# Mixture-of-experts kernel on one core: the arms for an expert's second and third token block are reordered, their jumps are hinted on TensorE, and an unused operand is no longer written

## The chip, the cores and the metric

The kernel runs on one core of one Trainium2 chip. The metric is the device time of one execution in microseconds (us), lower is better.

## What is computed

The reference is a two-layer diffusion backbone over 1024 latent and 256 context tokens of width 1024. Each layer does token mixing (gated linear attention, differential attention, pooling) and then a mixture of 16 experts. Only the experts matter here: every token goes to two experts of one group, and each expert is a gated feed-forward net.

```python
def expert_block(args):
    xblk, e = args
    return (jax.nn.silu(xblk @ w1[e]) * (xblk @ w3[e])) @ w2[e]
...
out = jnp.zeros((n_tok + 1, d), h.dtype).at[slot_tok].add(yb * slot_w[:, None])
```

How many tokens an expert gets is known only at run time, since the router decides it from the data.

## The kernel before

**Experts.** One stage per layer goes through the 16 experts in the order `eo`, written out one after the other in the program. An expert's weights come as 12 units of 128x1024. SyncE loads each (`fetch`, 8 buffers ahead), ScalarE copies it into the first half of a buffer `ew` and VectorE, or GpSimd for every third unit, subtracts to get the low part in the second half (L1579 and L1581, in `load_unit`); `ew` has 13 buffers. All matmuls are done three times, with high and low parts (`mm3`, L67 to L69).

**Token blocks.** Tokens are taken in blocks of 128. Block 0 always runs (`block` on `x0`: 72 matmuls of 128x512). Blocks 1 and 2 depend on the count `cnt` of the expert, which each engine loads into a register (L1814, L1872): a second block up to 64 tokens goes through `block_half`, a larger one through `block`; the same holds for the third. A loop follows for more than 384 tokens.

**Order.** The arms of an expert run before its block 0. Inside block 0, at the steps `side(u)`, the 12 weight units of the next expert are loaded, each when TensorE has let go of a unit of this expert, and the next expert's token blocks are gathered and prepared (`prep`). So an expert with at most 128 tokens has two blocks 0 in a row on TensorE. Here an expert is called N (none of the arms runs), H (half block), F (one full block) or T (a full block and a half block); the layers have the orders T and N in turn first, more N and H later. By the scatters and blocks in the trace, of 32 experts 16 are N, 7 H, 2 F and 7 T.

**Branches.** Each engine runs its own copy of the branches. In the program the code of an arm that is skipped lies between the branch and its target:

```python
with tc.If(cnt > P + P // 2) as big:      # L1822
    ...                                   # block 1; L1832: third block, full; L1834: loop
    with big2.Else():                     # L1853
        with tc.If(cnt > 2 * P):          # L1854: third block, half
with big.Else():
    with tc.If(cnt > P):                  # L1857: second block, half
        block_half(...)
```

So an N expert jumps at L1822 over everything up to the `Else`, and there at L1857 over the half block. An H expert jumps at L1822 and then runs the half block.

**Preparation.** `prep` transposes a block of tokens on TensorE, splits it into high and low parts (`split`, ScalarE and VectorE at L63 and L64), and on VectorE writes the low part of the first 64 tokens once more beside the high part (L1611). Only `block_half` reads that copy.

Of the kernel before, what the change touches and what calls it, by code (L numbers as in the profile page):

```python
# [20 lines left out]
P = 128  # L21
D = 1024
KD = D // P
NCTX = 256
# [31 lines left out]
def backbone_kernel(ctx: ExitStack, tc: tile.TileContext, x, ctx_in, cond, w_mod, b_mod, norm1, norm2, w_in_t, w_in_vg,  # L56
                    w_in_vd, w_out, wa2, gla_norm, lam_v, diff_norm, pool_w, pool_scale, router_w, router_b,
                    experts, final_norm, consts, rope, slot0, levels, edges, out, dbg=None, depth=DEPTH):
    nc = tc.nc
# [88 lines left out]
    for l in range(depth):  # L148
        last = l == DEPTH - 1
# [1403 lines left out]
        with ExitStack() as st:  # L1553
# [5 lines left out]
            early = True  # L1559
            xg2 = mp1.tile([P, D], F32, name="xg2")  # L1560
            g2b = {}
            for c in ((0,) if last else (0, 1)):
# [37 lines left out]
                fetch()  # L1600
            xt_ = [[mp1.tile([P, KD, n], F32R, name=f"x{n}{i}") for n in (P + P // 2, P)] for i in range(3)]

            def prep(g, xt):
                xh, xl = xt[0][:, :, P // 2:], xt[1]

                def half(j, tag="xtp"):
                    tp = pm_.tile([P, 4, P], F32, name="xtp", tag=tag, bufs=1 if tag == "xtp" else 2)
                    for i in range(4):
                        nc.tensor.transpose(tp[:, i, :], g[:, (4 * j + i) * P:(4 * j + i + 1) * P], ident)
                    split(xh[:, 4 * j:4 * j + 4, :], xl[:, 4 * j:4 * j + 4, :], tp)  # L1610
                    nc.vector.tensor_tensor(out=xt[0][:, 4 * j:4 * j + 4, 0:P // 2], in0=tp[:, :, 0:P // 2],  # L1611
                                            in1=xh[:, 4 * j:4 * j + 4, 0:P // 2].bitcast(F32), op=OP.subtract)
                return half

            def gain(n, w, wc):
# [112 lines left out]
            def col(e, b):  # L1728
                return slice(b * NE + e, b * NE + e + 1)

            def idle(u):
                pass

            for b in (1, 0):
                pf = prep(gg[b], xt_[2 * b])
                pf(0, ("hps", "xtp")[b])
                pf(1, ("hpse", "hpse")[b])
            units += [load_unit(u) for u in range(7, NUNIT)]
# [72 lines left out]
                        out_op(j)  # L1811
                    nc.sync.dma_start(out=out[P + 7 * P:2 * P + 7 * P, :], in_=X[7])

            cnt = nc.values_load(cnt_i[0:1, eo[0]:eo[0] + 1], min_val=0, max_val=cap)  # L1814
            gg[0] = gather(ix[:, col(eo[1], 0)], "xg0")
            gg[1] = gather(ix[:, col(eo[1], 1)], "xg1")
            if early:
                nc.gpsimd.indirect_dma_start(out=xg2, out_offset=None, in_=h2s,
                                             in_offset=bass.IndirectOffsetOnAxis(ap=ix[:, col(eo[0], 2)], axis=0))
            for ei, e in enumerate(eo):  # L1820
                x0, x1, x2 = xt_[ei % 2], xt_[2], xt_[(ei + 1) % 2]
                with tc.If(cnt > P + P // 2) as big:  # L1822
                    if not early:
                        nc.gpsimd.indirect_dma_start(out=xg2, out_offset=None, in_=h2s,
                                                     in_offset=bass.IndirectOffsetOnAxis(ap=ix[:, col(e, 2)], axis=0))
                    p2 = prep(xg2, x2)

                    def side1(u):
                        if u in (10, 11):
                            p2(u - 10, ("xtp", "hpse")[u - 10])  # L1830
                    block(x1, units, sw[:, col(e, 1)], swc[:, col(e, 1)], yx[:, col(e, 1)], side1, "e")
                    with tc.If(cnt > 2 * P + P // 2) as big2:  # L1832
                        block(x2, units, sw[:, col(e, 2)], swc[:, col(e, 2)], yx[:, col(e, 2)], idle, "e")
                        with tc.If(cnt > 3 * P):  # L1834
                            for t in tiles:
                                for j in range(2):
                                    nc.gpsimd.indirect_dma_start(
                                        out=slots, out_offset=bass.IndirectOffsetOnAxis(ap=di[:, t, j:j + 1], axis=0),
                                        in_=sva[:, t, j, 1:4], in_offset=None)
                            with tc.For_i(e * cap + 3 * P, e * cap + cnt, P) as i:  # L1840
                                sd = wk.tile([P, 3], F32, name="sd", tag="sd", bufs=1)
                                nc.sync.dma_start(out=sd, in_=slots[bass.ds(i, P), :])
                                si = wk.tile([P, 2], I32, name="si", tag="si", bufs=1)
                                nc.vector.tensor_copy(out=si, in_=sd[:, 0:2])
                                p3 = prep(gather(si[:, 0:1], "yt"), x1)
                                p3(0)
                                p3(1)
                                if not last:
                                    nc.vector.tensor_scalar(out=sd[:, 0:1], in0=sd[:, 0:1], scalar1=float(NCTX), scalar2=None, op0=OP.is_lt)
                                    nc.vector.tensor_tensor(out=sd[:, 1:2], in0=sd[:, 0:1], in1=sd[:, 2:3], op=OP.mult)  # L1850
                                    nc.vector.tensor_tensor(out=sd[:, 2:3], in0=sd[:, 2:3], in1=sd[:, 1:2], op=OP.subtract)
                                block(x1, units, sd[:, 2:3], sd[:, 1:2], si[:, 1:2], idle, "e")
                    with big2.Else():  # L1853
                        with tc.If(cnt > 2 * P):  # L1854
                            block_half(x2, units, sw[:, col(e, 2)], swc[:, col(e, 2)], yx[:, col(e, 2)])
                with big.Else():
                    with tc.If(cnt > P):  # L1857
                        block_half(x1, units, sw[:, col(e, 1)], swc[:, col(e, 1)], yx[:, col(e, 1)])
                nxt = []
                nx = {}  # L1860

                def side(u):
                    if ei + 1 == NE:
                        return
# [3 lines left out]
                    if early and u == 1:  # L1868
# [155 lines left out]
```

## Time and profile before

| what | value |
|---|---|
| runs (3) | median 2896.91 us, 2889.07 to 2903.89 |
| the profiled execution | 2908.22 us, span 2906.5 us |
| TensorE busy | 2539.1 us, 87% |
| VectorE busy | 1816.5 us, 63% |
| ScalarE busy | 1241.8 us, 43% |
| GpSimd busy | 898.9 us, 31% |
| mean granted TensorE clock | 0.934 |
| mean DMA rate | 170 GB/s |

The span is the time from the first to the last instruction of the profiled execution. Busy shares are means over stages with different limits, and a matmul at half clock counts as busy for twice as long.

### The profile page before, as it was taken

The numbers are of one execution on the slowest core, as the hardware profiler recorded it, in microseconds if no ns is written. First come the engines' busy times: TensorE is split into PE (matmuls) and PEld (weight loads), VectorE is DVE, ScalarE is ACT, GpSimd is POOL, SyncE is SP. The second block draws the span as 40 slices with busy tenths as digits, with TensorE's granted clock in tenths as the row PEclk, the third lists the DMA queues.
The fourth block names the chain that finished last, engine by engine and source line by source line (L and its number), as shares of the span: only waits on it lengthen the run. The fifth ranks groups of instructions, "written<-read, shape, count | busy, mean of one in ns | idle before, by whom it ended". The sixth has DMA issues, their size and how long they took to land. (4 is left out here: it accounts for less than half of the span.)

```text
span 2906.5 us, 41486 instructions
## 1 busy us (share of the span) xinstructions
PE 2539.1 (87%) x15412; PEld 2132.5 (73%) x15412; DVE 1816.5 (63%) x3175; ACT 1241.8 (43%) x2060; POOL 898.9 (31%) x576
## 2 busy tenths in 40 slices
PE   6999998898896899889887999979989788878875
PEld 3878887787785677667766898868978666656664
DVE  3304765777478667766775227748857866656765
ACT  3322213566234555544554232137743354545443
POOL 0000113302245444544540001122014445545452
PEclk8999999999897999989998999989989899989987
DMA  8373128331225666776774342173122568686765
GB/s 291 126 246 123 70 86 200 64 71 44 103 109 213 226 223 220 256 252 202 244 243 161 125 141 88 70 181 84 37 89 102 224 222 285 202 279 232 249 234 182
DMA packets 159573, 494.06 MB, mean 170 GB/s; under 512 B 18896, under 2 KB 40016, under 8 KB 158768
## 3 DMA queue, kind: packets, MB, share of 16 engines
q1 hardware_dynamic: 110336, 361.14, 37.5%
q0 software_dynamic: 29312, 99.39, 11.8%
q10 hardware_dynamic: 19552, 28.84, 2.7%
q8 instruction: 200, 3.28, 0.5%
q14 instruction: 173, 1.42, 0.2%
HBM read 408.75 MB, written 79.15 MB: 168 GB/s over the span
## 5 line engine op out<-in xcount | busy, mean ns | idle before, releaser
L1581 DVE TENSOR_TENSOR ew<-eraw,ew 128x1024 fp32r<-128x1024 f32 x256 | 433.7, 1713 | 65.2 <-ACT ew L1579 60.1
L1579 ACT ACTIVATE ew<-eraw 128x1024 fp32r<-128x1024 f32 x384 | 390.5, 1054 | 132.4 <-PE hps L69 115.0
L67 PE MATMUL hps<-ew,x 128*128 128x512 f32 x656 | 281.9, 430 | 105.2 <-PEq L1857 100.6
L1581 POOL TENSOR_TENSOR ew<-eraw,ew 128x1024 fp32r<-128x1024 f32 x128 | 334.4, 2622 | 61.1 <-ACT ew L1579 36.1
L212 PE MATMUL ps<-hh,w 128*128 128x256 f32 x2096 | 289.3, 292 | 17.9 <-ACT hh L319 4.7
L212 PEld LDWEIGHTS ps<-hh,w 128*128 128x128 f32 x2096 | 269.0, 197 | 27.7 <-issue 7.9
L69 PE MATMUL hps<-ew,x 128*128 128x512 f32 x656 | 271.2, 413 | 8.3 <-DVE x L64 7.6
L68 PE MATMUL hps<-ew,x 128*128 128x512 f32 x656 | 271.8, 414 | 0.0
L962 DVE TENSOR_REDUCE mx<-S 128x1 f32<-128x1280 f32 (+1 forms) x144 | 196.8, 1370 | 108.2 <-PE S L957 106.8
L1627 POOL DMA_INDIRECT xb<-yt,yx x54 | 131.2, 2430 | 368.6 <-DVE yt L1626 206.0
L67 PEld LDWEIGHTS hps<-ew,x 128*128 128x128 f32 x656 | 132.6, 202 | 139.7 <-issue 105.7
L970 ACT ACTIVATE pe<-S,mx 128x1280 f32<-128x1280 f32 (+1 forms) x144 | 177.4, 1232 | 49.2 <-DVE mx L962 41.2
L956 PE MATMUL S<-kk,qh 128*128 128x512 f32 (+1 forms) x400 | 159.0, 398 | 16.7 <-DMA qh<-qs 8.3
L69 PEld LDWEIGHTS hps<-ew,x 128*128 128x128 f32 x656 | 132.2, 202 | 41.7 <-DVE x L64 10.2
L68 PEld LDWEIGHTS hps<-ew,x 128*128 128x128 f32 x656 | 133.2, 203 | 28.2 <-issue 1.1
L212 PE MATMUL ps<-hl,w 128*128 128x256 f32 x1048 | 149.1, 286 | 0.0
L67 PE MATMUL ps<-wv,hh 128*128 128x256 f32 (+1 forms) x480 | 142.3, 296 | 0.0
L957 PE MATMUL S<-kk,ql 128*128 128x512 f32 (+1 forms) x400 | 141.4, 368 | 0.3 <-DMA ql<-qs 0.3
L69 PE MATMUL yps<-ew,ghl 128*128 128x512 f32 x328 | 132.5, 404 | 8.0 <-DVE ghl L64 8.0
L67 PE MATMUL yps<-ew,ghl 128*128 128x512 f32 x328 | 138.4, 422 | 0.0
L69 PE MATMUL ps<-wv,hl 128*128 128x256 f32 (+1 forms) x480 | 138.1, 288 | 0.0
L68 PE MATMUL ps<-wv,hh 128*128 128x256 f32 (+1 forms) x480 | 137.9, 287 | 0.0
(597 smaller groups left out, 5765.1 us busy)
## 6 DMA issues: line engine op xcount, KB each, us to landing
eraw<-in_experts_dram SPq DMA_DIRECT2D x384, 512.0 KB
s<-in_w_mod_dram SPq DMA_DIRECT2D x91, 512.0 KB
raw<-in_w_in_t_dram SPq DMA_DIRECT2D x28, 512.0 KB
xb<-xt POOLq DMA_DIRECT2D x18, 512.0 KB, 2.9
h2s<-tm POOLq DMA_DIRECT2D x18, 512.0 KB, 2.9
kk<-ks SPq DMA_DIRECT2D x14, 640.0 KB
ks<-shl ACTq DMA_DIRECT2D x16, 512.0 KB
qs<-shl ACTq DMA_DIRECT2D x16, 512.0 KB
```

What stands on the lines that cost most here:

```text
L67: nc.tensor.matmul(o, lhsT=lh, rhs=rh, start=start, stop=False)
L68: nc.tensor.matmul(o, lhsT=lh, rhs=rl, start=False, stop=False)
L69: nc.tensor.matmul(o, lhsT=ll, rhs=rh, start=False, stop=stop)
L212: nc.tensor.matmul(ps[:, o:o + 256], lhsT=wt[:, w_, k, :], rhs=h_[ci][:, k, :], start=w_ == 0 and h_ is hh and k == 0, stop=h_ is hl and k ...
L956: nc.tensor.matmul(S[:, j, :n], lhsT=qh[:, m, q1], rhs=kk[:, m, k0:k0 + n], start=True, stop=False)
L957: nc.tensor.matmul(S[:, j, :n], lhsT=ql[:, m, q1], rhs=kk[:, m, k0:k0 + n], start=False, stop=True)
L962: nc.vector.tensor_reduce(out=u["mx", m], in_=u["S", m], axis=AX.X, op=OP.max, negate=True)
L970: nc.scalar.activation(out=pe[:, :nk], in_=u["S", m], func=AF.Exp, bias=u["mx", m], scale=1.0, accum_out=acc)
L1579: nc.scalar.activation(out=w[:, 0, :], in_=raw, func=AF.Copy)
L1581: eng.tensor_tensor(out=w[:, 1, :], in0=raw, in1=w[:, 0, :].bitcast(F32), op=OP.subtract)
L1627: nc.gpsimd.indirect_dma_start(out=xb, out_offset=bass.IndirectOffsetOnAxis(ap=yidx[0:n], axis=0), in_=yt[0:n], in_offset=None, compute_op ...
```

## The change

The arms become one row of compares that all run in the order of the program. `any` (`cnt > P`) encloses them; then comes the half block under `cnt <= P + P // 2`, and behind it the full block under `cnt > P + P // 2` (label `big`). The third block is done the same way (labels `more` and `third`). The far jumps get hints, on TensorE alone: `aim` puts an instruction BRANCH_PREFETCH_HINT ahead of the branch with that label. Where it is given a comparison, a register instruction computes it first, and a value of 0 says that the branch will be taken. The hint for `any` of the next expert stands in block 0 after the sixth unit, that for the first expert before the first transposes; there the load of `cnt` moves too. `prep` leaves out the copy at L1611 for block 0 and in the loop.

```diff
-            def prep(g, xt):
+            def prep(g, xt, both=True):
...
-                    nc.vector.tensor_tensor(out=xt[0][:, 4 * j:4 * j + 4, 0:P // 2], in0=tp[:, :, 0:P // 2],
-                                            in1=xh[:, 4 * j:4 * j + 4, 0:P // 2].bitcast(F32), op=OP.subtract)
+                    if both:
+                        nc.vector.tensor_tensor(out=xt[0][:, 4 * j:4 * j + 4, 0:P // 2], in0=tp[:, :, 0:P // 2],
+                                                in1=xh[:, 4 * j:4 * j + 4, 0:P // 2].bitcast(F32), op=OP.subtract)
...
+            def aim(name, hint):
+                tc.mark_branch_hint_location(name, hint=hint, engines=(mybir.EngineType.PE,))
+
+            cnt = nc.values_load(cnt_i[0:1, eo[0]:eo[0] + 1], min_val=0, max_val=cap)
+            aim(f"any{l}_0", cnt > P)
             for b in (1, 0):
-                pf = prep(gg[b], xt_[2 * b])
+                pf = prep(gg[b], xt_[2 * b], b > 0)
...
-            cnt = nc.values_load(cnt_i[0:1, eo[0]:eo[0] + 1], min_val=0, max_val=cap)
...
-                with tc.If(cnt > P + P // 2) as big:
...
-                    with tc.If(cnt > 2 * P + P // 2) as big2:
...
-                    with big2.Else():
-                        with tc.If(cnt > 2 * P):
-                            block_half(x2, units, sw[:, col(e, 2)], swc[:, col(e, 2)], yx[:, col(e, 2)])
-                with big.Else():
-                    with tc.If(cnt > P):
+                with tc.If(cnt > P, label=f"any{l}_{ei}"):
+                    with tc.If(cnt <= P + P // 2):
+                        aim(f"big{l}_{ei}", "LikelyTaken")
                         block_half(x1, units, sw[:, col(e, 1)], swc[:, col(e, 1)], yx[:, col(e, 1)])
+                    with tc.If(cnt > P + P // 2, label=f"big{l}_{ei}"):
+                        aim(f"more{l}_{ei}", cnt > 2 * P)
+                        p2 = prep(xg2, x2)
...
+                        block(x1, units, sw[:, col(e, 1)], swc[:, col(e, 1)], yx[:, col(e, 1)], side1, "e")
+                        with tc.If(cnt > 2 * P, label=f"more{l}_{ei}"):
+                            with tc.If(cnt <= 2 * P + P // 2):
+                                aim(f"third{l}_{ei}", "LikelyTaken")
+                                block_half(x2, units, sw[:, col(e, 2)], swc[:, col(e, 2)], yx[:, col(e, 2)])
+                            with tc.If(cnt > 2 * P + P // 2, label=f"third{l}_{ei}"):
+                                block(x2, units, sw[:, col(e, 2)], swc[:, col(e, 2)], yx[:, col(e, 2)], idle, "e")
...
                     if u == 0:
                         nx["c"] = nc.values_load(cnt_i[0:1, f:f + 1], min_val=0, max_val=cap)
+                    if u == 5:
+                        aim(f"any{l}_{ei + 1}", nx["c"] > P)
...
-                            nx["p"] = prep(gg[j], (x2, x1)[j])
+                            nx["p"] = prep(gg[j], (x2, x1)[j], j > 0)
```

On TensorE at the start of the first layer's expert stage, before (`cnt_i` holds the counts, `xg` the gathered tokens, `hps` the first matmuls' sums):

```order
L1538 MATMUL small<-eacc,onesb 128x16
L1609 MATMUL xtp<-cs,xg 128x128 x16
L1814 TENSOR_LOAD cnt_i
L1822 COMPARE_AND_BRANCH
L67 MATMUL hps<-ew,x_11589 128x512
```

The same place in the changed kernel:

```order
L1538 MATMUL small<-eacc,onesb 128x16
L1737 TENSOR_LOAD cnt_i
L1735 REGISTER_ALU
L2025 BRANCH_PREFETCH_HINT
L1608 MATMUL xtp<-cs,xg 128x128 x16
L1825 COMPARE_AND_BRANCH
L1826 COMPARE_AND_BRANCH
L2025 BRANCH_PREFETCH_HINT
L1686 MATMUL hps<-ew,x_11589 128x512
```

The load of the count and the hint now stand ahead of the transposes, and the half block (L1686) follows the branches where the full block (L67) did.

On TensorE at the end of an expert's arms, where block 0 of the same expert follows, before (L1854 ends the third half block, L1857 branches around the second half block):

```order
L1687 MATMUL yps<-ew,gx 64x512
L1689 MATMUL yps<-ew,gx 128x512
L1854 UNCONDITIONAL_BRANCH x2
L1857 COMPARE_AND_BRANCH
L1686 MATMUL hps<-ew,x_11589 128x512
```

The same place in the changed kernel, behind the loop for more than 384 tokens, and the sixth unit of block 0 in it:

```order
L1843 UNCONDITIONAL_BRANCH
L1841 UNCONDITIONAL_BRANCH
L1837 UNCONDITIONAL_BRANCH
L1829 UNCONDITIONAL_BRANCH
L1825 UNCONDITIONAL_BRANCH
L67 MATMUL hps<-ew,x_11587 128x512
```

```order
L1637 MATMUL gtp<-cs,g 128x128 x2
L1735 REGISTER_ALU
L2025 BRANCH_PREFETCH_HINT
L67 MATMUL hps<-ew,x_11585 128x512
L68 MATMUL hps<-ew,x_11585 128x512
```

No arm is left between the target of `any` and block 0, and two instructions of the sequencer are new inside each block 0.

On VectorE in the preparation of the first expert's two blocks, before (block 1 in `x_11589` and `x_11590`, block 0 in `x_11585` and `x_11586`):

```order
L64 TENSOR_TENSOR x_11590<-xtp,x_11589 128x512
L1611 TENSOR_TENSOR x_11589<-xtp,x_11589 128x4x64
L64 TENSOR_TENSOR x_11586<-xtp,x_11585 128x512
L1611 TENSOR_TENSOR x_11585<-xtp,x_11585 128x4x64
L64 TENSOR_TENSOR x_11586<-xtp,x_11585 128x512
L1611 TENSOR_TENSOR x_11585<-xtp,x_11585 128x4x64
```

The same place in the changed kernel:

```order
L64 TENSOR_TENSOR x_11590<-xtp,x_11589 128x512
L1611 TENSOR_TENSOR x_11589<-xtp,x_11589 128x4x64
L64 TENSOR_TENSOR x_11590<-xtp,x_11589 128x512
L1611 TENSOR_TENSOR x_11589<-xtp,x_11589 128x4x64
L64 TENSOR_TENSOR x_11586<-xtp,x_11585 128x512 x2
```

The two copies for block 0 are gone; those for block 1 stay.

## Rows read from the trace of the kernel before

**Rows 1.** The page, first part: span, and busy time of engines.
```profile
span 2906.5 us, 41486 instructions
PE 2539.1 (87%) x15412; PEld 2132.5 (73%) x15412; DVE 1816.5 (63%) x3175; ACT 1241.8 (43%) x2060; POOL 898.9 (31%) x576
```

**Rows 2.** Waits of TensorE: waiter, releaser, us in total, times, longest.
```profile
PE hps L67 <- PEq L1857: 100.6, 16, 10.4
...
PE hps L1686 <- DVE ew L1581: 14.7, 4, 4.4
...
PE hps L1686 <- DVE yt L1624: 6.6, 2, 3.3
```

**Rows 3.** Instructions of line L1822: count, duration in ns min/median/max, start.
```profile
L1822 PEldq COMPARE_BRANCH  x32: 70/6219/7857, 929.1 to 2850.1; - x32
...
L1822 DVEq COMPARE_BRANCH  x32: 43/56/69, 941.8 to 2853.9; - x32
```

**Rows 4.** Instructions of line L1857 on TensorE's sequencer, same columns.
```profile
L1857 PEldq COMPARE_BRANCH  x30: 82/232/6301, 933.4 to 2853.7; - x30
```

**Rows 5.** Instructions of line L1832 on TensorE's sequencer.
```profile
L1832 PEldq COMPARE_BRANCH  x9: 330/365/3562, 979.6 to 2746.1; - x9
```

**Rows 6.** Line L1854: which waits it ended (us, times).
```profile
  PE hps L67: 3.7, 2
```

**Rows 7.** Timeline from 1167 us: start, length, engine, idle before and releaser.
```profile
1167.76 0.19 PEld L69 LDWEIGHTS yps<-ew,ghl 128*128 128x128 f32 x1 [0.40 <-DVE ghl L64]
...
1169.96 0.39 PE L69 MATMUL yps<-ew,ghl 128*128 128x512 f32 x1
...
1175.81 4.72 DVE L1581 TENSOR_TENSOR ew<-eraw,ew 128x1024 fp32r<-128x1024 f32 x1 [0.23 <-DVEq L1857]
1176.50 2.94 POOL L1581 TENSOR_TENSOR ew<-eraw,ew 128x1024 fp32r<-128x1024 f32 x1
...
1180.76 0.77 PE L67 MATMUL hps<-ew,x 128*128 128x512 f32 x1 [10.41 <-PEq L1857]
...
1181.75 0.63 PE L69 MATMUL hps<-ew,x 128*128 128x512 f32 x1
...
1186.39 0.39 PE L69 MATMUL hps<-ew,x 128*128 128x512 f32 x1
```

**Rows 8.** Windows, undisturbed blocks: us, busy of engines, clock, DMA share, GB/s.
```profile
1219.06:1238.17 19.11, 19.11 (x93) 15.27 (x91) 16.84 (x22) 15.20 (x22) 13.96 (x6) 1.00 0.62 188
1060.05:1072.88 12.83, 12.83 (x69) 9.49 (x70) 5.40 (x13) 4.75 (x11) 1.57 (x1) 1.00 0.29 43
```

**Rows 9.** Windows, six N experts, first layer: one, and their sum.
```profile
1091.81:1119.90 28.09, 21.86 (x93) 17.61 (x94) 25.36 (x20) 18.16 (x24) 17.73 (x10) 0.90 0.90 324
...
sum 173.33, PE 129.56 PEld 104.19 DVE 139.21 ACT 100.53 POOL 99.45; mean PE 21.59 PEld 17.36 DVE 23.20 ACT 16.75 POOL 16.57
```

**Rows 10.** Windows, seven N experts of the second layer.
```profile
2394.59:2420.00 25.41, 20.81 (x92) 16.40 (x92) 21.76 (x17) 16.30 (x22) 16.43 (x9) 0.93 0.93 334
...
sum 205.96, PE 150.72 PEld 119.85 DVE 155.75 ACT 107.60 POOL 111.28; mean PE 21.53 PEld 17.12 DVE 22.25 ACT 15.37 POOL 15.90
```

**Rows 11.** The six of rows 9, up to VectorE's second write of `ghl`.
```profile
1091.81:1116.24 24.43, 18.26 (x82) 14.71 (x82) 21.70 (x20) 15.82 (x22) 14.25 (x8) 0.93 0.88 314
...
sum 154.24, PE 110.65 PEld 89.40 DVE 120.24 ACT 82.75 POOL 84.48; mean PE 18.44 PEld 14.90 DVE 20.04 ACT 13.79 POOL 14.08
```

**Rows 12.** The seven of rows 10, up to the same write.
```profile
sum 182.74, PE 127.67 PEld 102.62 DVE 133.09 ACT 85.64 POOL 94.80; mean PE 18.24 PEld 14.66 DVE 19.01 ACT 12.23 POOL 13.54
```

**Rows 13.** Waits between 1091.5 and 1120 us.
```profile
PE yps L69 <- DVE ghl L64: 2.2, 1, 2.2
```

**Rows 14.** Windows, seven H half blocks, each from the end of the block before.
```profile
1202.11:1219.22 17.11, 14.20 (x70) 10.57 (x70) 8.18 (x14) 6.17 (x13) 6.79 (x4) 0.90 0.73 224
...
sum 122.85, PE 99.66 PEld 73.44 DVE 50.03 ACT 32.92 POOL 44.93; mean PE 14.24 PEld 10.49 DVE 7.15 ACT 4.70 POOL 6.42
```

**Rows 15.** Instructions of line L1611.
```profile
L1611 DVE TENSOR_TENSOR x<-xtp,x x146: 405/414/418, 930.0 to 2852.8; 128x256 fp32r<-128x256 f32 x146
```

More of the change, by code (lines that the diff above doesn't have):

```diff
@@ L1558, in backbone_kernel @@
             YT = 3
-            early = True
             xg2 = mp1.tile([P, D], F32, name="xg2")
@@ L1812, in fix @@
                     nc.sync.dma_start(out=out[P + 7 * P:2 * P + 7 * P, :], in_=X[7])
-            cnt = nc.values_load(cnt_i[0:1, eo[0]:eo[0] + 1], min_val=0, max_val=cap)
             gg[0] = gather(ix[:, col(eo[1], 0)], "xg0")
             gg[1] = gather(ix[:, col(eo[1], 1)], "xg1")
-            if early:
-                nc.gpsimd.indirect_dma_start(out=xg2, out_offset=None, in_=h2s,
-                                             in_offset=bass.IndirectOffsetOnAxis(ap=ix[:, col(eo[0], 2)], axis=0))
+            nc.gpsimd.indirect_dma_start(out=xg2, out_offset=None, in_=h2s,
+                                         in_offset=bass.IndirectOffsetOnAxis(ap=ix[:, col(eo[0], 2)], axis=0))
@@ L1820, in backbone_kernel @@
             for ei, e in enumerate(eo):
                 x0, x1, x2 = xt_[ei % 2], xt_[2], xt_[(ei + 1) % 2]
-                with tc.If(cnt > P + P // 2) as big:
[L1823 to L1831, printed above, removed]
-                    with tc.If(cnt > 2 * P + P // 2) as big2:
[L1833 to L1852, printed above, removed]
-                    with big2.Else():
-                        with tc.If(cnt > 2 * P):
-                            block_half(x2, units, sw[:, col(e, 2)], swc[:, col(e, 2)], yx[:, col(e, 2)])
@@ L1856, in backbone_kernel, with side1 @@
-                with big.Else():
-                    with tc.If(cnt > P):
-                        block_half(x1, units, sw[:, col(e, 1)], swc[:, col(e, 1)], yx[:, col(e, 1)])
+                with tc.If(cnt > P, label=f"any{l}_{ei}"):
+                    with tc.If(cnt <= P + P // 2):
+                        aim(f"big{l}_{ei}", "LikelyTaken")
+                        block_half(x1, units, sw[:, col(e, 1)], swc[:, col(e, 1)], yx[:, col(e, 1)])
+                    with tc.If(cnt > P + P // 2, label=f"big{l}_{ei}"):
+                        aim(f"more{l}_{ei}", cnt > 2 * P)
+                        p2 = prep(xg2, x2)
+                        def side1(u):
+                            if u in (10, 11):
+                                p2(u - 10, ("xtp", "hpse")[u - 10])
+                        block(x1, units, sw[:, col(e, 1)], swc[:, col(e, 1)], yx[:, col(e, 1)], side1, "e")
[5 more added lines that the diff above has]
+                                block(x2, units, sw[:, col(e, 2)], swc[:, col(e, 2)], yx[:, col(e, 2)], idle, "e")
+                                with tc.If(cnt > 3 * P):
+                                    for t in tiles:
+                                        for j in range(2):
+                                            nc.gpsimd.indirect_dma_start(
+                                                out=slots, out_offset=bass.IndirectOffsetOnAxis(ap=di[:, t, j:j + 1], axis=0),
+                                                in_=sva[:, t, j, 1:4], in_offset=None)
+                                    with tc.For_i(e * cap + 3 * P, e * cap + cnt, P) as i:
+                                        sd = wk.tile([P, 3], F32, name="sd", tag="sd", bufs=1)
+                                        nc.sync.dma_start(out=sd, in_=slots[bass.ds(i, P), :])
+                                        si = wk.tile([P, 2], I32, name="si", tag="si", bufs=1)
+                                        nc.vector.tensor_copy(out=si, in_=sd[:, 0:2])
+                                        p3 = prep(gather(si[:, 0:1], "yt"), x1, False)
+                                        p3(0)
+                                        p3(1)
+                                        if not last:
+                                            nc.vector.tensor_scalar(out=sd[:, 0:1], in0=sd[:, 0:1], scalar1=float(NCTX), scalar2=None, op0=OP.is_lt)
+                                            nc.vector.tensor_tensor(out=sd[:, 1:2], in0=sd[:, 0:1], in1=sd[:, 2:3], op=OP.mult)
+                                            nc.vector.tensor_tensor(out=sd[:, 2:3], in0=sd[:, 2:3], in1=sd[:, 1:2], op=OP.subtract)
+                                        block(x1, units, sd[:, 2:3], sd[:, 1:2], si[:, 1:2], idle, "e")
@@ L1867, in side @@
                         nxt.append(load_unit(len(nxt)))
-                    if early and u == 1:
+                    if u == 1:
                         nc.gpsimd.indirect_dma_start(out=xg2, out_offset=None, in_=h2s,
```

## The prediction

> **What bounds the kernel now.** I read the page first: TensorE is busy for 87% of the span [rows 1], so its idle time is what the other engines can give back. The list of its waits then names the largest one that no data explains: 100.6 us in 16 waits before the first matmul of a block 0, put down to TensorE's own sequencer at the branch of L1857 [rows 2]. The instructions of that branch and of L1822 show why. On TensorE's sequencer the compare of L1822 takes 70 ns when it falls through and 6.2 us at the median, 7.9 us at most; on VectorE the same compare takes 56 ns [rows 3]. The second jump of an N expert, L1857, takes between 82 ns and 6.3 us [rows 4]. A jump over the third block, about half as far, takes from 0.33 us to 3.56 us, 0.365 us at the median [rows 5]. So a far jump is dear on TensorE alone, and its price depends on where it lands. I read that as the fetch of code that TensorE does not hold yet.
>
> The timeline shows what of it is seen [rows 7]. The last matmul of a block 0 ends at 1170.35 us (1169.96 and 0.39), and TensorE stands still for 10.41 us. Its queue had work for the first microseconds of the jumps, so a jump of 0.3 us costs nothing and one of 6 us costs about 3.5 to 4.5. [...]
>
> An undisturbed block 0 takes 19.11 us at full clock, a half block 12.83 us [rows 8]. Six N experts of the first layer take 173.33 us from the end of one block 0 to the end of the next, that is 28.9 us each; seven of the second layer take 205.96 us, 29.4 us each [rows 9, 10]. Both are some 10 us above 19.11 us. Seven H half blocks with the pause ahead of them take 122.85 us [rows 14], against 7 times 12.83 = 89.8 us.
>
> **Part by part.** *Compares in a row, with hints.* An N expert then has one jump, of `any`, and its target is the start of block 0. Of an H expert the jump comes behind its half block instead of ahead of it. The hint for `any` stands after the sixth of 12 units of the block 0 before, some 10 us ahead of the branch (6 of the 12 units of 19.11 us are left, and transposes). The hints for `big` and `third` stand ahead of a half block, 12.83 us, that for `more` ahead of a full block. A jump takes 7.9 us at most [rows 3], so a fetch that starts at the hint is done by then. The first expert's hint now stands ahead of the transposes, which themselves wait for gathered tokens, so it is early too. No row shows a hinted jump that was taken. Its price lies between 0.07 us (the compare that falls through) and the full 6.2 us; I take 0.35 us, the median of the cheap jumps in rows 5, and the queue hides that.
>
> *What N experts get back.* If TensorE starts at once, VectorE becomes what it waits for. Inside block 0 VectorE must have written the second `ghl` (low part of the gated product) before the last quarter of the block, and in its order the weight loads and the output of the block before stand ahead of this. Of a block 0 without a pause ahead, that point comes 19.11 - 2.6 = 16.5 us after the start (in rows 7 the wait for `ghl` at 1167.76 us, 2.6 us ahead of the end at 1170.35 us). From the end of the block 0 before to the second `ghl`, VectorE is busy for 20.04 us in the mean of the first layer's six and 19.01 us in the second layer's seven [rows 11, 12]; ops of 1.2 us take up to 4.7 us while GpSimd subtracts too [rows 7], and that stays. The change takes off two copies of 0.41 us, 0.82 us [rows 15]. VectorE's idle time on this way is not all to be had, since loads wait for units that TensorE lets go: the most packed case has 24.43 - 21.70 = 2.7 us of it [rows 11]. I take 2.0 us. So the second `ghl` is ready after 20.04 - 0.82 + 2.0 = 21.2 us, and 20.2 us in the second layer; TensorE waits 4.7 and 3.7 us in the block. A wait can lower the clock again: a half block after a pause of some 3 us ran at a mean clock of 0.90 over 17.1 us, 1.7 us lost [rows 14]. I add half of that, 0.9 us. An N expert then takes 19.11 + 4.7 + 0.9 = 24.7 us and 23.7 us. Saved: 6 x (28.9 - 24.7) = 25 us and 7 x (29.4 - 23.7) = 40 us. Such a wait is there already in one of them, 2.2 us [rows 13]. The three other N experts, the first of the first layer and the last of each, I count at 3 us each, half of the mean pause of 100.6/16 = 6.3 us, since less is loaded behind them: 9 us.
>
> *H experts.* 122.85 - 7 x (12.83 + 0.35) = 30.6 us, pause and half clock together. The waits before them are put down to VectorE [rows 2], but its writes at that time are those of other operands, so I take the jump as the cause.
>
> *F experts.* The waits behind L1854 are 3.7 us in two [rows 6]; with the lower clock behind the longer one I take 5 us.
>
> *T and F, the jump over the half block.* New on their way, without a hint: nine jumps over the code of one half block, less than half as far as those of rows 5. Bounds: nothing, as five of nine there took 0.33 to 0.37 us, hidden by the queue; and 3.56 us each, of which some 1 us would be seen, 9 us in all. I take nothing. The branches out of the nested arms, at most five in a row, are cheap when near: 82 to 232 ns [rows 4], hidden too.
>
> *Copies left out.* 64 of 146 go, 26 us of VectorE [rows 15]. Outside N experts VectorE has room in block 0 (16.84 of 19.11 us [rows 8]), so nothing is counted there; with N experts it is in the sum already.
>
> *Other engines.* Their compares keep to tens of ns [rows 3], and the new ones are as near. *DMA.* In N experts it is at a share of 0.90 to 0.93 and 324 to 334 GB/s [rows 9, 10], and a shorter N expert asks for the same weights sooner. Eight weight buffers lie ready, and the arms between let the queue catch up (a share of 0.29 in a half block [rows 8]). I take 3 us off; if it bound fully, an N expert would take about 26 us (25.4 us at 334 GB/s in rows 10 is the shortest).
>
> **Sum.** 25 + 40 + 9 + 30.6 + 5 - 3 = 107 us. The profiled execution took 2908.2 us (span 2906.5 us), so it would be 2801 us. Against the median of the runs, 2896.9 us, that is 2790 us.
>
> **Rivals.** *The freed time is eaten up.* TensorE gets its code in time, but DMA or VectorE keep N experts at 26 us: 379.3 - 13 x 26 = 41 us saved, with 9, 31 and 5 us of the rest 86 us: 2811 us. For it speaks the DMA share, against it the idle DMA in the arms.
>
> *The opposite:* VectorE's holds shrink as GpSimd falls elsewhere, N experts reach 21 us: 379.3 - 13 x 21 = 106 us, with the rest 150 us: 2747 us.
>
> *The hints do nothing.* Then H experts pay as before, only later. N experts keep one jump: those with two dear ones fall to the time of those with one. The 13 have a mean of 29.2 us, and those with one dear jump take 25.4 to 28.1 us, about 27 [rows 9, 10]; if six have two, these take (379.3 - 7 x 27)/6 = 31.7 us, and 6 x 4.7 = 28 us are saved, with the second jumps of the first and last expert some 6 us more: 34 us, 2863 us. No row shows a hint at work, so this has a chance of its own.
>
> [...]
>
> **Chances and range.** Forecast 0.64; eaten up 0.12; deeper gain 0.07; no effect of hints 0.11; slower 0.04; no change at all 0.02. The forecast's own range is 2760 to 2825 us, from VectorE's idle time of 0 to 2.7 us, no clock loss or 1.7 us in each, and 0 to 9 us for the half-block jumps. Over all cases 2750 to 2850 us leaves out the two last and most of the case without effect. About 0.5% (14.5 us) is what a measurement of this kernel tells from no change: faster 0.93, same 0.03, slower 0.04.
>
> **What will show it.** On TensorE's sequencer the compare of `any` (L1825) at N experts takes under 0.5 us in place of 6.2 us, and the 100.6 us at its first matmul are gone; if they stay, hints do nothing. The compare of `big` (L1829) behind half blocks is as short. N experts take 22 to 26 us, with waits for `g` or `ghl` from VectorE of 3 to 5 us in them; the DMA share in them is above 0.90. [...] The copies at L1611 number 82. The clock over half blocks of H experts is at 1.00. The prediction is wrong in size if the waits for VectorE come out at 1 us or at 8 us, or if jumps over the half block are dear.

## The result and the profile after

The changed kernel is slower: 2978.05 us (median of 4 runs, 2966.06 to 2984.5) against 2894.02 us of the kernel before beside it, a ratio of 1.028 [1.024, 1.033]. The prediction was 2790 us, faster with a chance of 0.93. The profiled execution took 2966.06 us.

The page, first part, of the changed kernel, beside [rows 1]:

```profile
span 2964.3 us, 41767 instructions
PE 2547.3 (86%) x15412; PEld 2128.2 (72%) x15412; DVE 1886.3 (64%) x3111; ACT 1248.5 (42%) x2060; POOL 864.1 (29%) x576
```

TensorE's waits in the changed kernel, beside [rows 2]:

```profile
PE hps L67 <- DVEq L1826: 73.1, 9, 9.7
PE gtp L1637 <- DVE g L1655: 58.4, 15, 4.3
PE yps L69 <- DVE ghl L64: 38.7, 27, 2.1
...
PE hps L1686 <- DVE x L1611: 12.3, 5, 2.5
```

The 100.6 us for TensorE's own sequencer are gone. In their place stand 73.1 us for VectorE's sequencer at L1826, the compare of the second block's half, nine times: two F and seven T experts. Another 97 us are waits for VectorE's products inside blocks.

The branches L1825 (`any`), L1826 (half block) and L1829 (`big`) in the changed kernel, on TensorE's sequencer (PEldq) and VectorE's (DVEq), beside [rows 3] and [rows 4]:

```profile
L1825 PEldq COMPARE_BRANCH  x32: 81/214/1347, 919.4 to 2911.8; - x32
...
L1826 PEldq COMPARE_BRANCH  x23: 67/211/364, 945.3 to 2865.7; - x23
...
L1826 DVEq EVENT_SEMAPHORE  x9: 21/21/21, 957.8 to 2793.8; - x9
...
L1829 PEldq COMPARE_BRANCH  x23: 68/189/391, 948.8 to 2866.9; - x23
```

The hints work, but the medians of these rows mix jumps with compares that fall through (0.07 to 0.09 us) and branches at the end of an arm that ran (0.19 to 0.21 us). Taken one by one from the same trace, the 16 N experts' jumps at L1825 take 0.34 to 0.38 us, but for the first with 1.35 us; at L1822 before, they took 3.5 to 7.9 us. The nine jumps over the half block at L1826 are cheap too, 0.23 to 0.36 us. The row on VectorE is what I had not priced: where an arm is skipped, VectorE runs a semaphore instruction in its place, nine times, and it runs it when it gets there.

When it gets there is in the timeline, at the start of the second T expert:

```profile
1039.28 0.40 PE L69 MATMUL yps<-ew,ghl 128*128 128x512 f32 x1
1047.70 0.76 PE L67 MATMUL hps<-ew,x 128*128 128x512 f32 x1 [8.02 <-DVEq L1826]
1048.26 0.63 PE L68 MATMUL hps<-ew,x 128*128 128x512 f32 x1
...
1040.96 0.68 DVE L64 TENSOR_TENSOR x<-xtp,x 128x512 fp32r<-128x512 f32 x1
...
1042.82 1.27 DVE L1619 SCALAR_TENSOR_TENSOR yt<-g,sw,yt 128x1024 f32<-128x1024 f32 x1
...
1046.28 1.21 DVE L1580 TENSOR_TENSOR ew<-eraw,ew 128x1024 fp32r<-128x1024 f32 x1
```

TensorE ends block 0 at 1039.68 us. VectorE then still has the tail of that block to do: token splits, `gain`, the output and two weight units, up to 1047.49 us. Only then does it pass the skipped half block, and the first matmul of block 1 starts 0.2 us later, at a granted clock of 0.50 up to 1050 us: there a matmul takes 0.63 us and one starts every 0.43 us, where from 1051 us on, at 1.00, it takes 0.39 us and one starts every 0.23 us.

Windows of the six N experts of the first layer, columns as in [rows 9]:

```profile
1101.24:1129.05 27.81, 21.19 (x92) 16.52 (x92) 25.20 (x21) 16.17 (x22) 16.40 (x9) 0.94 0.90 305
...
sum 164.13, PE 128.43 PEld 99.87 DVE 146.91 ACT 94.61 POOL 94.97; mean PE 21.40 PEld 16.64 DVE 24.48 ACT 15.77 POOL 15.83
```

They take 27.4 us each; 24.7 was predicted. TensorE is busy for 21.4 us of them (the mean clock is 0.88 to 0.94) and idle for 6.0 us. VectorE is busy for 24.48 us in each, more than the 23.20 us of [rows 9], though it has less to do.

Adding up each expert from the end of the block 0 before to the end of its own, over both layers (worked out from the matmuls in the traces; the first expert of a layer counts from VectorE's write of the counts; "outside" is the rest of the span), gives this ledger in us. It is of one profiled execution of each kernel, and also has the kernels of the experiments:

| kernel | N | H | F | T | outside | runs, median |
|---|---|---|---|---|---|---|
| before | 458.8 | 255.6 | 107.5 | 360.2 | 1724.4 | 2894 to 2898 |
| after | 426.3 | 273.1 | 115.4 | 438.9 | 1710.6 | 2978.05 |
| e1_nohint | 425.1 | 290.9 | 116.6 | 442.3 | 1720.2 | 2994.05 |
| e2_buf | 448.5 | 289.3 | 102.7 | 374.5 | 1719.7 | 2936.82 |
| e3_else | 424.3 | 256.2 | 107.0 | 357.2 | 1724.4 | 2879.91 |
| e12_full_first | 403.9 | 306.0 | 102.2 | 392.8 | 1725.4 | 2947.86 |
| e4_hints_only | 418.1 | 243.2 | 104.3 | 356.0 | 1721.7 | 2846.44 |
| e5_copies | 450.2 | 250.5 | 106.9 | 356.7 | 1725.3 | 2892.23 |
| e8_hints_copies | 417.6 | 244.2 | 103.6 | 361.0 | 1725.5 | 2847.90 |
| e6_novg | 342.6 | 231.4 | 107.4 | 411.1 | 1725.4 | 2817.44 |
| e11_novg_nohint | 368.0 | 270.9 | 108.0 | 434.1 | 1727.6 | 2904.55 |
| e9_vec_only | 425.5 | 247.4 | 94.8 | 352.9 | 1719.3 | 2840.90 |
| e10_else_vec | 356.4 | 255.3 | 88.8 | 347.5 | 1724.1 | 2772.15 |
| e7_hints_vec | 369.6 | 228.0 | 88.6 | 351.0 | 1719.9 | 2761.28 |

From before to after, N gains 32.5 us, and T loses 78.7, H 17.5 and F 7.9 us: 71.6 us lost in the experts. The profiled execution of the changed kernel is 14 us shorter outside them, which no other kernel repeats, and it is the shortest of its four runs: so the two profiled executions lie 58 us apart where the medians lie 84 us apart.

### The profile page after: what moved, and what is told of

The parts are those of the page before. It is cut to its first block, busy times and chain, and to the rows that moved or that the text cites. A ratio compares the mean times of both kernels' runs of the same rounds, so it can differ in the third digit from the quotient of the medians.

```text
span 2964.3 us, 41767 instructions
## 1 busy us (share of the span) xinstructions
PE 2547.3 (86%) x15412; PEld 2128.2 (72%) x15412; DVE 1886.3 (64%) x3111; ACT 1248.5 (42%) x2060; POOL 864.1 (29%) x576
## 3 DMA queue, kind: packets, MB, share of 16 engines
q0 software_dynamic: 29312, 99.39, 12.4%
## 5 line engine op out<-in xcount | busy, mean ns | idle before, releaser
L1580 DVE TENSOR_TENSOR ew<-eraw,ew 128x1024 fp32r<-128x1024 f32 x256 | 523.3, 2066 | 36.5 <-ACT ew L1578 32.1
L67 PE MATMUL hps<-ew,x 128*128 128x512 f32 x656 | 285.3, 435 | 82.6 <-DVEq L1826 73.1
L1580 POOL TENSOR_TENSOR ew<-eraw,ew 128x1024 fp32r<-128x1024 f32 x128 | 328.0, 2575 | 15.2 <-ACT ew L1578 12.7
L212 PE MATMUL ps<-hh,w 128*128 128x256 f32 x2096 | 285.9, 290 | 17.7 <-ACT hh L319 5.2
L68 PE MATMUL hps<-ew,x 128*128 128x512 f32 x656 | 272.5, 415 | 0.0
L69 PE MATMUL hps<-ew,x 128*128 128x512 f32 x656 | 271.2, 413 | 0.2 <-DVE x L64 0.2
L1627 POOL DMA_INDIRECT xb<-yt,yx x54 | 105.7, 1957 | 475.3 <-DVE yt L1626 174.5
L67 PEld LDWEIGHTS hps<-ew,x 128*128 128x128 f32 x656 | 134.2, 205 | 126.1 <-issue 99.2
L956 PE MATMUL S<-kk,qh 128*128 128x512 f32 (+1 forms) x400 | 156.9, 392 | 19.1 <-ACT pe L970 9.8
L69 PE MATMUL yps<-ew,ghl 128*128 128x512 f32 x328 | 134.0, 408 | 38.7 <-DVE ghl L64 38.7
L69 PEld LDWEIGHTS hps<-ew,x 128*128 128x128 f32 x656 | 132.6, 202 | 32.9 <-DVE x L64 0.9
L68 PEld LDWEIGHTS hps<-ew,x 128*128 128x128 f32 x656 | 133.6, 204 | 26.1
L67 PE MATMUL ps<-wv,hh 128*128 128x256 f32 (+1 forms) x480 | 142.1, 296 | 0.0
L67 PE MATMUL yps<-ew,ghl 128*128 128x512 f32 x328 | 138.1, 421 | 0.0
L69 PE MATMUL ps<-wv,hl 128*128 128x256 f32 (+1 forms) x480 | 138.0, 288 | 0.0
L68 PE MATMUL ps<-wv,hh 128*128 128x256 f32 (+1 forms) x480 | 137.8, 287 | 0.0
```

The lines of the kernel that those rows point to most:

```text
L67: nc.tensor.matmul(o, lhsT=lh, rhs=rh, start=start, stop=False)
L68: nc.tensor.matmul(o, lhsT=lh, rhs=rl, start=False, stop=False)
L69: nc.tensor.matmul(o, lhsT=ll, rhs=rh, start=False, stop=stop)
L212: nc.tensor.matmul(ps[:, o:o + 256], lhsT=wt[:, w_, k, :], rhs=h_[ci][:, k, :], start=w_ == 0 and h_ is hh and k == 0, stop=h_ is hl and k ...
L956: nc.tensor.matmul(S[:, j, :n], lhsT=qh[:, m, q1], rhs=kk[:, m, k0:k0 + n], start=True, stop=False)
L1580: eng.tensor_tensor(out=w[:, 1, :], in0=raw, in1=w[:, 0, :].bitcast(F32), op=OP.subtract)
```

## The experiments

The theory (A): hints bring the code in time, but the row of compares makes T and F experts wait for VectorE, and VectorE, held up by GpSimd (V), eats up what N experts gain. The rival (B): hints themselves cost, so the time falls without them.

**e1_nohint.** All hints out.

```diff
             def aim(name, hint):
-                tc.mark_branch_hint_location(name, hint=hint, engines=(mybir.EngineType.PE,))
+                pass
```

> The changed kernel with all hints left out, the compares still in a row. Theory A (the hints do their work; the loss is TensorE waiting for VectorE to pass the skipped half block in T and F experts, 73.1 us in 9 waits, plus the half clock behind it): the 73 us stay, and the far jumps come back, 6.2 us on TensorE's sequencer at N experts and behind the half block of H experts; of each some 2 to 4 us are seen: 2978 + 23 x 3 = about 3045 us, at least 2990. [...]

Measured: 2994.05 us, ratio 1.033 [1.029, 1.038]. B falls. So does A's size: hints are worth some 16 us in this kernel, not 67 (the four runs of each kernel do not overlap). Its waits of TensorE:

```profile
PE hps L67 <- DVEq L1826: 58.1, 9, 9.8
PE yps L69 <- DVE ghl L64: 37.5, 15, 5.1
PE hps L67 <- PEq L1825: 29.9, 14, 3.9
...
PE hps L67 <- PEq L1829: 23.5, 7, 3.6
...
PE hps L67 <- PEq L1841: 14.3, 7, 3.4
...
PE gtp L1637 <- DVE g L1655: 8.2, 5, 3.2
```

The jumps cost 29.9 + 23.5 + 14.3 = 67.7 us, as they should. But the three waits for VectorE fall from 73.1 + 58.4 + 38.7 = 170.2 us to 58.1 + 37.5 + 8.2 = 103.8 us. What TensorE loses at the jump it does not wait for later. N experts take the same, 425.1 against 426.3 us, though their jumps now take 3.5 to 6.9 us.

**e2_buf.** The full block 1 on block 0's buffers, so that it shares none of `hps`, `g` and `ghl` with the half block.

```diff
-                        block(x1, units, ..., yx[:, col(e, 1)], side1, "e")
+                        block(x1, units, ..., yx[:, col(e, 1)], side1, "")
```

> The changed kernel, with the full block 1 on the buffers of block 0 (hps, g, ghl) in place of those that it shares with the half block ahead of it. Theory A: TensorE's first matmul of block 1 needs nothing of the skipped half block any more, so most of the 73.1 us in 9 waits at L1826 goes; a part of about 1 us each comes back at the first product g, for which VectorE has to be there 7 us into the block: 2978 - 65 - 10 (less half clock) = about 2905 us. Rival B (hints cost): unchanged, 2978 us. A middle result, 2930 to 2960 us, would say that the same wait moves to the next place where VectorE is needed.

Measured: 2936.82 us, ratio 1.015 [1.011, 1.018], the middle result. Its waits of TensorE:

```profile
PE hps L67 <- DVEq L1825: 97.2, 16, 11.1
PE hps L67 <- DVEq L1829: 30.2, 7, 4.4
```

The nine waits at L1826 are gone and T experts fall by 64.4 us. Now block 0 shares its buffers with an arm ahead of it, so it waits in each of the 16 N and 7 H experts until VectorE has passed the skipped full block. The wait follows the shared buffers, which is theory A's mechanism.

**e3_else.** The arms as alternatives again, inside `any`, the third block likewise; the hints of `big` and `third` go.

```diff
-                    with tc.If(cnt <= P + P // 2):
-                        ...
-                    with tc.If(cnt > P + P // 2, label=f"big{l}_{ei}"):
+                    with tc.If(cnt > P + P // 2, label=f"big{l}_{ei}") as big:
                         ...
+                    with big.Else():
+                        block_half(x1, ...)
```

> The changed kernel with the order of arms of before inside the enclosing compare any: full block first, half block in its Else, the third block likewise; the hint of any stays, those of big and third are gone. Theory A: the wait of T and F experts at the skipped half block goes (73 us and some 10 us of half clock), H experts pay a far jump without hint ahead of their half block, as before (some 3 us more than now, 7 times): 2978 - 83 + 21 = about 2916 us. Rival B (hints cost, 32 of the 55 are still there): 2978 - 23 x 1.5 = about 2940 us, and the waits inside blocks stay.

Measured: 2879.91 us, ratio 0.995 [0.992, 0.998]: 98 us less than the changed kernel, and 36 us less than forecast. T experts are at 357.2 us, as low as before the change, and no wait for VectorE at a branch is left. H experts gain 17 us though their far jump has no hint, which I had not expected: the row had cost them more than the jump does.

**e12_full_first.** The row kept, with the full block's arm ahead of the half block's; the hint of `big` goes.

```diff
                 with tc.If(cnt > P, label=f"any{l}_{ei}"):
-                    with tc.If(cnt <= P + P // 2):
-                        aim(f"big{l}_{ei}", "LikelyTaken")
-                        block_half(x1, ...)
                     with tc.If(cnt > P + P // 2, label=f"big{l}_{ei}"):
                         ...
+                    with tc.If(cnt <= P + P // 2):
+                        block_half(x1, ...)
```

> The changed kernel with the row of compares the other way round: the full block's arm first, the half block's behind it (the hint of any stays; that of big is gone). Theory A (an arm that runs waits, by the buffers that it shares, for VectorE to pass the skipped arm ahead of it): T and F experts lose their 73 us and 10 us of half clock, and H experts' first matmul now waits for VectorE past the skipped full arm, 7 times up to 8 us less the 2.4 us that five of them wait already: 2978 - 83 + 45 = about 2940 us, with a new wait at L1686 put down to VectorE's sequencer, 7 times. If a row of compares costs T and F the same in either order, 2970 us or more.

Measured: 2947.86 us, ratio 1.019 [1.015, 1.022]. The wait has changed over to the H experts, seven times:

```profile
PE hps L1686 <- DVEq L1826: 33.8, 7, 6.6
```

H experts take 306.0 us, the most of all kernels; T experts fall by 46.1 us. They keep a part of their loss: block 0 now stands behind the skipped half block (L1859), and waits there for 26.7 us in nine:

```profile
L1859 PEldq COMPARE_BRANCH  x32: 74/215/2731, 994.1 to 2835.0; - x32
...
  PE hps L67: 26.7, 9
```

That is not VectorE: in eight of the nine, block 0 starts 0.7 to 1.7 us before VectorE comes to L1859. It is TensorE's own way past this arm, which has no hint: in eight of nine the jump there, or the branch behind it, takes 1.8 to 2.7 us. So a jump over a half block is not cheap everywhere. N experts are 22 us shorter than in the changed kernel, which this theory does not explain.

**e4_hints_only.** The kernel before, with hints and nothing else of the change; its far jump is the branch `big`.

```diff
+            cnt = nc.values_load(cnt_i[0:1, eo[0]:eo[0] + 1], min_val=0, max_val=cap)
+            aim(f"big{l}_0", cnt > P + P // 2)
...
-                with tc.If(cnt > P + P // 2) as big:
+                with tc.If(cnt > P + P // 2, label=f"big{l}_{ei}") as big:
+                    aim(f"third{l}_{ei}", cnt > 2 * P + P // 2)
...
+                    if u == 5:
+                        aim(f"big{l}_{ei + 1}", nx["c"] > P + P // 2)
```

> The kernel before with hints alone: the far jump of L1822 is hinted at the sixth unit of the block 0 ahead of it, and that to the third block's half; the arms and the copies at L1611 stay. Theory A: the 100.6 us at L1857 go, T and F experts are as before, N experts take 27.3 us as in the changed kernel in place of 28.9 and 29.4 us (25 us saved), H experts lose their jump (15 us), others 5 us: 2894 - 45 = about 2850 us. Rival B (hints cost about 2 us each): 2894 + 32 x 2 - 50 or more = 2900 to 2960 us.

Measured: 2846.44 us, ratio 0.983 [0.979, 0.987], as forecast. 41 hints save 51 us. Of its waits at jumps one is left, the second jump of N experts (over the half block, without a hint), dear in five cases:

```profile
PE hps L67 <- PEq L1862: 23.5, 5, 6.8
```

**e5_copies** and **e8_hints_copies.** The copies at L1611 for block 0 left out, in the kernel before and in e4.

```diff
-                            nx["p"] = prep(gg[j], (x2, x1)[j])
+                            nx["p"] = prep(gg[j], (x2, x1)[j], j > 0)
```

> The kernel before with one part of the change alone: the copies at L1611 for block 0 are left out. By the prediction's term they are worth 0.82 us of VectorE in an N expert whose block 0 is bound by VectorE, and nothing elsewhere: 0 to 13 us, I expect 2890 us, not to be told from before. A theory that the copies matter by their place (VectorE lets TensorE go on earlier at the end of each block 0) would give 32 x 0.8 = 26 us or more: 2870 us or less.

> The kernel before with hints, and without the copies at L1611 for block 0: the changed kernel's parts but for the compares in a row. Theory A: all that the change loses comes from the compares in a row, so this is as fast as hints alone or some us better, 2835 to 2846 us. If another part of the change costs something too, it is above 2860 us.

Measured: 2892.23 us, ratio 0.998 [0.996, 1.001], and 2847.90 us, ratio 0.982 [0.976, 0.988]. The copies do nothing that can be told. All parts but the row of compares together give e8; the row, with its own hints, turns it into the changed kernel and costs 130 us.

**e6_novg.** The changed kernel with the weight subtractions on VectorE, all but four: the first expert of each layer names GpSimd for two units elsewhere, and these stay.

```diff
-                eng = eng or (nc.gpsimd if u % 3 == 2 else nc.vector)
+                eng = eng or nc.vector
```

> The changed kernel with all weight subtractions on VectorE, none on GpSimd. Theory V (N experts stay at 27 us since GpSimd's subtractions hold those of VectorE, whose 256 take 523 us in place of 256 x 1.21 = 310 us): VectorE then needs 384 x 1.21 = 465 us for all, 58 us less, most of it in N experts, 2 us each: 2978 - 32 = about 2946 us, and no subtraction takes over 1.5 us. Rival (VectorE is short of time anyway, and four more subtractions in each expert make it worse): N experts take 28 us or more, 2978 to 3000 us. The 73 us at the skipped half block should stay within 15 us in both.

Measured: 2817.44 us, ratio 0.972 [0.966, 0.978]. V's direction was right and its size five times too small: 161 us. The wait at L1826 stays:

```profile
PE hps L67 <- DVEq L1826: 57.3, 9, 7.7
```

The subtractions on VectorE in the changed kernel, as a group by line (count, busy us, mean ns):

```profile
L1580 DVE TENSOR_TENSOR ew<-eraw,ew 128x1024 fp32r<-128x1024 f32 x256 | 523.3, 2066 | 36.5 <-ACT ew L1578 32.1 <-DVEq L1825 3.5 <-DVEq L1841 0.8
```

and in e6:

```profile
L1580 DVE TENSOR_TENSOR ew<-eraw,ew 128x1024 fp32r<-128x1024 f32 x380 | 458.6, 1236 | 31.6 <-ACT ew L1578 24.9 <-DVEq L1825 3.5 <-issue 1.3
```

VectorE does a half more of them (380 of 384) and is busy with them for 65 us less. Three still take over 1.5 us. The same six N experts in windows of e6:

```profile
1096.13:1117.28 21.15, 19.44 (x92) 15.28 (x92) 20.52 (x25) 16.11 (x22) 6.79 (x4) 1.00 1.02 361
...
sum 126.96, PE 116.63 PEld 92.03 DVE 123.13 ACT 96.47 POOL 37.04; mean PE 19.44 PEld 15.34 DVE 20.52 ACT 16.08 POOL 6.17
```

They take 21.2 us in place of 27.4: VectorE is busy for 4.0 us less in each, and TensorE for 2.0 us less, since its granted clock stays at 1.00, where it was 0.88 to 0.94. I had counted only the first of the two, and only for the subtractions.

**e7_hints_vec** and **e9_vec_only.** The same line, on e4 and on the kernel before.

> The kernel before with hints alone, and with all weight subtractions on VectorE. There VectorE's 256 subtractions take 463 us, as much as 384 x 1.21 = 465 us, so by theory V VectorE's time stays and only its holds of 3 to 6 us go: 2846 us less 0 to 20. By the rival more work on VectorE lengthens N experts by about 1 us each: 2860 us or more.

> The kernel before with all weight subtractions on VectorE and nothing else. If the holds of VectorE by GpSimd were what N experts wait for, whatever the jumps, this gains as much as in the changed kernel, some 85 to 160 us: 2740 to 2810 us. If each of the two, jump and hold, covers the other (theory V: hints gave 51 us with the holds in place, and the holds 85 us behind hints), it gains less: 2897 - 85 + 40 = about 2850 us, with the 100 us at L1857 still there.

Measured: 2761.28 us, ratio 0.954 [0.948, 0.960], the fastest of all, and 2840.90 us, ratio 0.981 [0.978, 0.984]. In e7 my expectation was too small again, for the same two reasons. In e9 the jumps are still paid:

```profile
PE hps L67 <- PEq L1857: 84.0, 16, 8.7
```

Alone, the hints give 51 us and the subtractions on VectorE 53 us; together 136 us. Each part hides some of what the other would give.

**e11_novg_nohint.** e6 without hints.

> The changed kernel with all weight subtractions on VectorE and without hints. With GpSimd's subtractions in place the hints gave 16 us (2994 against 2978). Theory V (freed time is eaten up by VectorE held by GpSimd): now the far jumps show in full, 16 N and 7 H experts at 3 to 4 us each and the half clock behind them: 2817 + 80 = about 2897 us. If the hints themselves are worth little whatever VectorE does, it is 2817 + 16 = 2833 us.

Measured: 2904.55 us, ratio 1.003 [1.001, 1.005]. The hints that gave 16 us in the changed kernel give 87 us once VectorE is not held: 25 us in N experts, 40 us in H and 23 us in T experts. This tells V from a theory of weak hints.

**e10_else_vec.** e3 with the subtractions on VectorE.

> The changed kernel with the arms as If and Else inside the enclosing compare any (as in e3) and all weight subtractions on VectorE (as in e6). Theory A: e6 less its 57 us at the skipped half block, and H experts with a far jump without a hint, some 15 us: 2817 - 57 - 5 + 15 = about 2770 us, and no wait of N experts at a jump. If the wait at the skipped half block hides work that is waited for anyhow, it stays near 2800 us.

Measured: 2772.15 us, ratio 0.957 [0.954, 0.960]. Against e6 the T experts are 63.6 us and the F experts 18.6 us shorter, 20 us more than theory A gave them. H experts are 23.9 us longer with a jump without a hint, where 15 us was expected, and N experts 13.8 us, where nothing was. The time is about 2 us from what theory A gave, and that is partly luck: the two misses cancel.

## Why the prediction was wrong

**Which step failed.** First the part "*T and F, the jump over the half block*". It priced the jump alone, bounded it by jumps, and took nothing. The jump is indeed nothing (0.23 to 0.36 us). But with compares in a row the full block follows the half block in the program and shares `hps`, `g` and `ghl` with it, so it waits until VectorE, the last, has been past the skipped arm. Before, the two were alternatives and neither was ahead of the other. VectorE comes there 8.1 us behind TensorE in the mean (73.1 us over nine), since the tail of a block 0 is its work. e2 moved the wait by moving the buffers, e12 by turning the row round, e3 removed it.

The 78.7 us of T experts are 57 us of this wait and 16 us in their block 0, which takes 21.4 us in the mean for 19.1 us and waits for `ghl` in all seven; the rest is short pauses and the lower clock. In the two F experts 17.7 us of the wait left a loss of 7.9 us; what they saved elsewhere was not followed. The longer block 0 is not a matter of the row alone: it takes 19.1 us in e6, where the row stays and GpSimd has only four subtractions left, and in e3, where GpSimd subtracts and the row is gone.

**N experts: the terms 25, 40 and 9 us were mis-sized,** 74 us in all against 32.5 measured. The mechanism was right, a wait for VectorE inside block 0: 55.2 us in 14 waits for `g` and 15.9 us in 13 for `ghl`, 4.4 us per N expert. In the six of the first layer TensorE is idle for 6.0 us, where 4.7 was taken, and at its lower mean clock it is busy for 2.3 us more than in an undisturbed block, where 0.9 was taken. The step took VectorE's busy time from the trace of before, with the holds by GpSimd of that trace ("and that stays"). They did not stay as they were: the group's mean is 2066 ns in the changed kernel, and in the kernel before, in the same view, it was 1713 ns:

```profile
L1581 DVE TENSOR_TENSOR ew<-eraw,ew 128x1024 fp32r<-128x1024 f32 x256 | 433.7, 1713 | 65.2 <-ACT ew L1579 60.1 <-DVEq L1857 4.5
```

Subtractions over 1.5 us rose from 58 to 76 of 256.

The rival "the freed time is eaten up" was right in kind, with 27.4 us for 26 us, and wrong about DMA: e6 takes 21 us at 361 GB/s, so DMA was no bound. e6 and e11 show that VectorE's holds are what ate it up. Where they are gone and the jumps hinted (e7), N experts gain 89 us, between the forecast's 74 and the deeper rival's 115 (106 for thirteen, and the same 9 for three); in e6 they gain 116 us.

**H experts: 30.6 us were forecast and 17.5 lost.** Two errors. The sum took an undisturbed half block of 12.83 us, but with the jump hinted alone (e4) the pause ahead falls from 3.0 to 0.1 us and the half block itself takes 15.7 us for 14.5, with waits for `g` inside: 12.4 us are left. I had dismissed the waits that the list put down to VectorE [rows 2]; in the changed kernel five of seven half blocks still wait 2.5 us for `x` at L1611. The other 30 us between e4 and the changed kernel are the row's: 18 of them lie in block 0 behind the skipped full block, 21.1 us for 19.1, with a wait for `ghl` in all seven. They shrink to 3 us between e7 and e6, so they come about through VectorE and GpSimd. How, in single steps, no run separates; GpSimd's own semaphore instructions in skipped arms are a candidate that I did not test.

**What held.** The hint of `any` brings the jump under 0.5 us in 15 of 16, and the 100.6 us went; hints without effect are out. Slower, given a chance of 0.04, came out, but not because hints cost: e1 and e4 show that they save time, 16 and 51 us. With 41 hints in e4 TensorE waits for its own issue in the middle of a group of matmuls (L69) for 3.6 us in all, and without any in e1 for 5.1 us (L68, L69). A jump's target can be fetched ahead: an N expert's jump takes 0.36 us at the median with a hint, and 3.5 to 6.9 us without in e1. The fetch itself is in the traces. In the kernel before, a packet of the instruction queue (q8 on the page, 200 packets in all) is under way within each of the 35 jumps of over 2 us at L1822, L1832 and L1857, and within none of the 36 compares there of under 0.4 us. In the changed kernel such a packet starts 3.1 to 4.0 us after the hint in 15 of the 16 N experts' cases, and 7.7 us after it in the first expert's; within 9 us of the other 16 hints of `any`, whose jumps are not taken, none starts. The copies at 82 changed nothing that can be told; the 3 us for DMA were not seen either, and its share in the six N experts is 0.84 to 0.92, where I had said above 0.90.

In sum, forecast 107 us saved; lost 71.6 us in the experts. The difference of 178 us is T 78.7, H 48.1, N 41.5, F 12.9, less 3 for DMA.

## What to carry to other kernels

When alternatives are turned into compares in a row, ask for each block that runs which skipped arm now stands ahead of it and shares a buffer with it: here it waited for the slowest engine to get past that arm, 8.1 us in the mean, however cheap the jump was (0.23 to 0.36 us). Before counting a freed pause as time, ask which engine is next, and take that engine's durations undisturbed and disturbed, since what it loses to a neighbour can grow when the work is packed closer, as here from 1713 to 2066 ns for a subtraction. Two waits that hide each other are tested together: hints and the moved subtractions gave 51 and 53 us alone, 136 us together.

## What was not expected of the hardware

A second engine made the pair slower: the expert stage was shorter with nearly all subtractions on VectorE. The timeline of the changed kernel, GpSimd's and VectorE's subtractions at the end of one block:

```profile
1030.85 4.75 POOL L1580 TENSOR_TENSOR ew<-eraw,ew 128x1024 fp32r<-128x1024 f32 x2
...
1037.55 2.40 POOL L1580 TENSOR_TENSOR ew<-eraw,ew 128x1024 fp32r<-128x1024 f32 x1
...
1032.96 3.72 DVE L1580 TENSOR_TENSOR ew<-eraw,ew 128x1024 fp32r<-128x1024 f32 x1 [0.53 <-ACT ew L1578]
...
1036.94 4.10 DVE L1580 TENSOR_TENSOR ew<-eraw,ew 128x1024 fp32r<-128x1024 f32 x1
```

VectorE's two end at 1036.68 and 1041.04 us, each 1.1 us behind the end of GpSimd's (1035.60 and 1039.95 us), about its own undisturbed 1.21 us: it stood still meanwhile. So it is throughout. All 76 of the changed kernel's subtractions on VectorE that take over 1.5 us began while GpSimd was at an instruction, and end 1.1 us behind the end of a subtraction of GpSimd's. One GpSimd subtraction of 2.4 us that delays VectorE by up to 2.9 us costs more than the 1.21 us it takes off. So VectorE stands still until GpSimd's subtraction has ended; by what means the one holds the other, no run shows. It was there to be read in [rows 7], where a subtraction took 4.72 us beside GpSimd's, and I left it standing as a constant.

A hint on TensorE takes 35 ns at the median. The instruction, 55 times in the changed kernel:

```profile
L2025 PEldq BRANCH_PREFETCH_HINT  x55: 28/35/50, 910.8 to 2901.3; - x55
```

And the compare of `any` without hints, in e1 (16 jumps of 3.5 to 6.9 us, and 16 compares that fall through):

```profile
L1825 PEldq COMPARE_BRANCH  x32: 70/1768/6879, 926.1 to 2940.8; - x32
```
